# Five widths of a gather table in a hybrid decoder step: 34, 47, 37, 30, 11 columns become 33, 45, 34, 28, 10

## The chip, the cores and the metric

The kernel runs on one core of one Trainium2 chip. The metric is the device time of one execution in microseconds (us). The time before is 3196.83 us, the median of three runs from 3183.53 to 3199.43 us. All arithmetic is in 32-bit floats; most matrix products are made of three products of a high and a low part.

## The reference, cut to what matters

The program computes one layer of a decoder trunk for 512 prompt tokens and 64 sample tokens (8 sequences of 8), each of 2048 channels. The first half (modulation, a recurrent head group, a short convolution, an output projection) isn't touched. The second half is a mixture of 16,384 single-neuron experts, PEER:

```python
q = (xb @ w_q).reshape(PEER_BLOCK, PEER_HEADS, 2, HALF_DIM)
sc = jnp.einsum('thpk,pnk->thpn', q, sub_keys)
v1, i1 = lax.top_k(sc[:, :, 0], 16); v2, i2 = lax.top_k(sc[:, :, 1], 16)
cand = v1[..., :, None] + v2[..., None, :]        # 256 sums per head
top, pos = lax.top_k(cand, 16)
eidx = (i1 * 128 + i2) at pos                     # the expert
g = softmax(top)
act = gelu(sum_d x[d] * expert_u[eidx][d]) * g
out = sum over the picks of act * expert_v[eidx]
```

Each token has 8 heads of 16 picks: 128 picks, each of an expert whose number is first key times 128 plus second key. A pick takes a row of 2048 numbers (8 KB) of `u` and one of `v`.

## The kernel before, in words

**Two ways to an expert.** The 128 first keys are ranked by how often they are likely to be chosen (`rank_keys`, line 935). The experts of the first 80 keys (`L`, line 32), 80 blocks of 128 experts, are computed densely for all 512 prompt tokens: every token by every expert, with a weight of zero where the token didn't pick it. The picks of the other 48 first keys are gathered row by row, as are all 128 picks of the sample tokens.

**Dense part.** In the U stage TensorE runs over the 160 halves of the 80 `u` blocks (`u_half`, line 1395; its matmuls are line 1405). In the V stage it runs over 80 steps of four blocks each (`v_column`, line 1413; matmuls at line 1425). SyncE loads the raw halves (lines 892 and 897). ScalarE makes the high part `xhi` (line 908), GpSimd the low part `xlo` (line 909), and TensorE needs both.

**Gathered part.** `count` (line 1058) counts each prompt token's rare picks. `sort` (line 1113) orders the 512 tokens by that count, most first. The sorted tokens are cut into five tiles by `SORTED` (line 40): a first place, a number of tokens, and a number c of columns. With the sample tokens as tile 0 (64 columns, all full) they make the table `GT` (line 816). A tile of 128 tokens has one token on each partition and c slots for each. The first and the last tile have 64 tokens; each has its first c slots on one partition and the next c on another, so its token has 2c slots. `slots` (line 1187) fills the slots of a tile by taking the largest codes eight at a time, in rounds of eight (`mr`, line 1193). A slot that no pick fills gets an index past the end of the expert table, and the gather leaves out such a row.

**One column, one gather, one dot or one add.** For every column of the table `take` (line 1234) issues on GpSimd one indirect DMA of up to 128 rows of 8 KB. In `gather_u` (line 1238) VectorE then multiplies the landed rows by the token's input, which lies in PSUM, and sums (line 1263); in `gather_v` (line 1272) it multiplies by the activation and adds to an accumulator in PSUM (line 1290, the first of a tile 1287, the last 1292). The rows land in five buffers in the U stage and seven in the V stage.

**Order.** The whole of this is in an order written out by hand. In the U stage the dots of a tile follow as its slots become ready, at a set rate (line 1684); from the step at which all slots are ready the rest, and 16 adds of tile 0 (`EARLY_V`), are spread evenly over the steps that are left (line 1695). In the V stage the other adds are spread over the steps by a sum of costs: a column of tile 0 counts 1.25, any other 1.0 (lines 1753 and 1765). The tiles of the V stage come in the order 0, 2, 1, 3, 5, 4 (line 1315).

**What does not fit.** A token with more rare picks than slots is counted in `flag`:

```python
for i, (p0, n, c) in enumerate(GT):
    cap = c * 128 // n if i else NPK
    V.tensor_scalar(srt[:, i, 0:1], srt[:, i, 0:1], -float(cap), 0.0, op0=ALU.add, op1=ALU.max)
```

If the sum isn't zero, a general path at the end of the program (line 1813) goes through all five tiles once more, with 128 gathers of `u` and 128 of `v` for each, by the same `take`, keeps only the picks that had no slot, and computes the output again.

Of the kernel before, what the change touches and what calls it, by code (L numbers as in the profile page):

```python
# [36 lines left out]
TC = 32  # L37
NCH = NA // TC
QT = NA // 128
SORTED = ((0, 64, 34), (64, 128, 47), (192, 128, 37), (320, 128, 30), (448, 64, 11))  # L40
RB = 5
RV = 7
ENDS = 3
# [38 lines left out]
def build(ctx, tc, A, O, dbg=None):  # L82
# [732 lines left out]

    GT = [(None, NG, NPK // 2)] + [(p0, n, c) for p0, n, c in SORTED]
    rows_i, gwt = {}, {}
# [369 lines left out]
    def slots(i):  # L1187
# [5 lines left out]
        mr = -(-m // 8) * 8  # L1193
        sb = pools["rs"].tile([128, max(2 * NPK, 3 * max(-(-c_ * 128 // n_ // 8) * 8 for _, n_, c_ in SORTED))], F32,
                              name=f"sl{i}", tag="sl", bufs=1)
# [746 lines left out]
```

## Time and profile before

| | |
|---|---|
| median of three runs | 3196.83 us |
| the profiled execution | 3192.57 us |
| its span, first to last instruction | 3190.7 us |
| mean granted TensorE clock | 0.984 |
| gathers of `u` and of `v` | 223 and 223 |
| U stage, by the trace | about 1197 to 2214 us |
| V stage, by the trace | about 2214 to 3168 us |

A share is busy time over the span. A wait names the instruction that stood idle, the one that ended its wait, the total, how often, and the longest. A row of a stretch gives start and end, then the busy time of each engine and its count of instructions, the granted TensorE clock (1.00 is full), the mean busy share of the 16 DMA engines (a little over 1.00 where records overlap) and what they moved.

### The profile page before, as it was taken

The numbers are of one execution on the slowest core, as the hardware profiler recorded it, in microseconds if no ns is written. First come the engines' busy times: TensorE is split into PE (matmuls) and PEld (weight loads), VectorE is DVE, ScalarE is ACT, GpSimd is POOL, SyncE is SP. The second block draws the span as 40 slices with busy tenths as digits, with TensorE's granted clock in tenths as the row PEclk, the third lists the DMA queues.
The fourth block names the chain that finished last, engine by engine and source line by source line (L and its number), as shares of the span: only waits on it lengthen the run. The fifth ranks groups of instructions, "written<-read, shape, count | busy, mean of one in ns | idle before, by whom it ended". The sixth has DMA issues, their size and how long they took to land.

```text
span 3190.7 us, 46633 instructions
## 1 busy us (share of the span) xinstructions
PE 3063.3 (96%) x17239; PEld 2604.8 (82%) x17239; DVE 2151.6 (67%) x3267; ACT 1045.4 (33%) x1640; POOL 1708.0 (54%) x1001
## 2 busy tenths in 40 slices
PE   6999999999989999999999999998999999999997
PEld 2788888889979998887888788886888888777776
DVE  3455521142245897977898999856677888788755
ACT  3244311122232232232655555542322222222122
POOL 2233333344334235666666666656767777768642
PEclk9999999999999999999999999999999999999998
DMA  9744566633332227889879898989999999899964
GB/s 391 279 137 138 177 215 215 205 121 132 130 121 90 70 83 247 307 312 399 339 309 402 354 400 354 403 281 357 395 376 383 401 341 367 329 397 344 368 245 155
DMA packets 297067, 882.84 MB, mean 277 GB/s; under 512 B 37590, under 2 KB 79446, under 8 KB 245366
## 3 DMA queue, kind: packets, MB, share of 16 engines
q1 hardware_dynamic: 160608, 380.39, 34.0%
q0 software_dynamic: 66336, 413.41, 32.5%
q10 hardware_dynamic: 69888, 86.00, 7.6%
q8 instruction: 136, 2.23, 0.3%
q14 instruction: 99, 0.81, 0.1%
HBM read 879.89 MB, written 66.81 MB: 297 GB/s over the span
## 4 chain that ended last, share of the span: by engine, by line
PE 74%; DMA 12%; DVE 5%; POOL 3%; issue 3%; ACT 1%; SPq 0%; ACTq 0%; POOLq 0%; DVEq 0%
PE pu L1405 20%; PE pv L1425 19%; PE pp_o L140 6%; DMA raw<-v 3%; PE pp_c L140 3%; PE pp_s L140 3%; PE qa L140 3%; PE pp_b L140 3%; PE qb L140 3%; DMA gsb<-gd 3%; PE pp_x L140 2%; PE pp_y L140 2%; PE ada L190 2%; PE gbank L1605 2%; DMA v<-v,rows 2%
## 5 line engine op out<-in xcount | busy, mean ns | idle before, releaser
L909 POOL TENSOR_TENSOR xlo<-raw,xhi 128x1024 fp32r<-128x1024 f32 x320 | 778.6, 2444 | 408.7 <-ACT xhi L908 403.0
L908 ACT ACTIVATE xhi<-raw 128x1024 fp32r<-128x1024 f32 x320 | 338.1, 1060 | 875.4 <-PE pv L1425 319.8
L1263 DVE SCALAR_TENSOR_TENSOR u<-u,hT 128x2048 f32<-128x2048 f32 x223 | 503.7, 2282 | 111.3 <-DMA u<-u,rows 110.0
L1290 DVE SCALAR_TENSOR_TENSOR accB<-v,dots,accB 128x2048 f32<-128x2048 f32 x211 | 496.5, 2353 | 109.4 <-DMA v<-v,rows 103.2
L1425 PE MATMUL pv<-ahi,xhi 128*128 128x512 f32 x1280 | 511.5, 400 | 23.1 <-ACT xhi L908 16.2
L1405 PE MATMUL pu<-hhi,xhi 128*128 128x512 f32 x1280 | 514.4, 402 | 0.0
L1425 PE MATMUL pv<-ahi,xlo 128*128 128x512 f32 x1280 | 508.3, 397 | 4.3 <-POOL xlo L909 4.3
L1425 PE MATMUL pv<-alo,xhi 128*128 128x512 f32 x1280 | 506.0, 395 | 0.0
L1405 PE MATMUL pu<-hhi,xlo 128*128 128x512 f32 x1280 | 502.7, 393 | 0.4 <-POOL xlo L909 0.3
L1405 PE MATMUL pu<-hlo,xhi 128*128 128x512 f32 x1280 | 502.9, 393 | 0.0
L1235 POOL DMA_INDIRECT u<-u,rows x223 | 224.8, 1008 | 211.1 <-DVE u L1263 142.4
L1425 PEld LDWEIGHTS pv<-ahi,xhi 128*128 128x128 f32 x1280 | 243.2, 190 | 80.5 <-ACT xhi L908 17.5
L1425 PEld LDWEIGHTS pv<-ahi,xlo 128*128 128x128 f32 x1280 | 243.1, 190 | 63.0 <-POOL xlo L909 6.2
L1425 PEld LDWEIGHTS pv<-alo,xhi 128*128 128x128 f32 x1280 | 243.6, 190 | 55.2
L1235 POOL DMA_INDIRECT v<-v,rows x223 | 258.1, 1157 | 54.7 <-issue 39.5
L1405 PEld LDWEIGHTS pu<-hhi,xlo 128*128 128x128 f32 x1280 | 240.8, 188 | 56.2 <-POOL xlo L909 2.1
L1405 PEld LDWEIGHTS pu<-hhi,xhi 128*128 128x128 f32 x1280 | 241.4, 189 | 49.4 <-issue 0.9
L1405 PEld LDWEIGHTS pu<-hlo,xhi 128*128 128x128 f32 x1280 | 241.5, 189 | 48.4
L1599 ACT ACTIVATE op<-op,it 128x128 f32<-128x128 f32 x512 | 155.3, 389 | 35.6 <-DVE op L1591 32.8
L1605 PEld LDWEIGHTS gbank<-wr,op 128*128 128x128 f32 x1024 | 133.5, 192 | 24.0 <-ACT stg L1612 15.0
L129 POOL TENSOR_TENSOR wlo_o<-raw_o,whi_o 128x1024 fp32r<-128x1024 f32 x32 | 77.6, 2425 | 119.7 <-ACT whi_o L127 119.7
L1447 DVE TENSOR_TENSOR acc<-acc,pv 128x512 f32<-128x512 f32 x144 | 96.4, 681 | 65.7 <-PE pv L1425 63.6
(498 smaller groups left out, 5439.4 us busy)
## 6 DMA issues: line engine op xcount, KB each, us to landing
wa<-w_ada SPq DMA_DIRECT2D x96, 1024.0 KB
raw<-ut SPq DMA_DIRECT2D x160, 512.0 KB
raw<-v SPq DMA_DIRECT2D x320, 256.0 KB
actd<-act ACTq DMA_DIRECT2D x80, 256.0 KB
gd<-stg ACTq DMA_DIRECT2D x64, 320.0 KB
gsb<-gd ACTq DMA_DIRECT2D x80, 256.0 KB
actr<-actd ACTq DMA_DIRECT2D x40, 512.0 KB
raw_o<-w_out SPq DMA_DIRECT2D x32, 512.0 KB
```

The lines of the kernel that those rows point to most:

```text
L129: lo_engine(share).tensor_sub(lo, raw, r32(hi))
L140: PE.matmul(o, st, mv[pick](k), start=first, stop=last)
L908: S.activation(hi, raw, AF.Copy)
L909: G.tensor_sub(lo, raw, r32(hi))
L1235: G.indirect_dma_start(out=out, out_offset=None, in_=src, in_offset=bass.IndirectOffsetOnAxis(ap=idx, axis=0), bounds_check=NE * 128 - 1, ...
L1263: V.scalar_tensor_tensor(r, r, 1.0, st["h"], op0=ALU.mult, op1=ALU.mult, accum_out=dots[i][:, j:j + 1])
L1290: V.scalar_tensor_tensor(st["a"], r, dots[i][:, j:j + 1], st["a"], op0=ALU.mult, op1=ALU.add)
L1405: PE.matmul(pu, st[:, kk, :], movA[mv](k), start=k == 0 and a == 0, stop=k == KD - 1 and a == 2)
L1425: PE.matmul(pv, st, mv, start=first and j == 0 and a == 0, stop=last and not end and j == SG - 1 and a == 2)
L1447: V.tensor_add(ak, ak, pv)
L1599: S.activation(ops[:, j0 + j, :], ops[:, j0 + j, :], AF.Copy, scale=it[2][:, b * 4 + j:b * 4 + j + 1])
L1605: PE.matmul(pg[:, j * L:(j + 1) * L], ops[:, j0 + j, :], wr[:, j0 + j, :], start=True, stop=True)
```

## The change

```diff
-SORTED = ((0, 64, 34), (64, 128, 47), (192, 128, 37), (320, 128, 30), (448, 64, 11))
+SORTED = ((0, 64, 33), (64, 128, 45), (192, 128, 34), (320, 128, 28), (448, 64, 10))
```

Each tile keeps its tokens and loses one, two, three, two and one column. The slots of a token go from 68, 47, 37, 30, 22 to 66, 45, 34, 28, 20. All loops over the columns, the counts `NU`, `NV0` and `NT` that pace the gathers, and the bound `cap` follow from the table. Nothing else is edited.

## The prediction

> **What bounds the kernel.** I read the page from the top: the span, the busy times, the chain that ended last.
>
> ```profile
> span 3190.7 us, 46633 instructions
> ...
> PE 3063.3 (96%) x17239; PEld 2604.8 (82%) x17239; DVE 2151.6 (67%) x3267; ACT 1045.4 (33%) x1640; POOL 1708.0 (54%) x1001
> ...
> PE 74%; DMA 12%; DVE 5%; POOL 3%; issue 3%; ACT 1%; SPq 0%; ACTq 0%; POOLq 0%; DVEq 0%
> ```
>
> TensorE is busy for 3063.3 of 3190.7 us and makes 74% of the chain; VectorE and GpSimd, from which the change takes work, are busy 67% and 54%. But an average hides stages, so next come TensorE's own waits from 1180 us to the end, where the gathers run (the rows of the last few microseconds left out).
>
> ```profile
> PE pv L1425 <- ACT xhi L908: 16.2, 3, 8.8
> PE gbank L1605 <- ACT stg L1612: 8.9, 11, 3.3
> PE pv L1425 <- DVE acc L1447: 6.2, 4, 2.7
> PE pv L1425 <- POOL xlo L909: 4.3, 3, 1.6
> ...
> PE pv L1425 <- issue: 0.7, 1, 0.7
> PE pu L1405 <- POOL xlo L909: 0.3, 1, 0.3
> ```
>
> No row names a gather, a dot (L1263) or an add (L1290). The U stage's matmuls lose 9.2 us in all (8.9 + 0.3), the V stage's 27.4 us (16.2 + 6.2 + 4.3 + 0.7). These 36.6 us, and what the clock loses behind them, are all that any relief elsewhere could win here. Where do they lie? The view by stretches, cut at the ends of the gather's tiles:
>
> ```profile
> core 0: us, PE busy (x) PEld busy (x) DVE busy (x) ACT busy (x) POOL busy (x), PEclk, DMA share, GB/s
> ...
> 1853.00:2214.00 361.00, 360.13 (x1810) 302.69 (x1809) 289.98 (x312) 180.00 (x372) 222.49 (x145) 1.00 0.93 364
> 2214.00:2457.00 243.00, 231.42 (x989) 187.12 (x988) 174.25 (x96) 65.51 (x68) 168.07 (x95) 0.97 0.99 377
> 2457.00:2635.00 178.00, 178.00 (x774) 144.91 (x773) 150.46 (x90) 41.33 (x37) 135.00 (x81) 1.00 0.98 374
> 2635.00:2762.00 127.00, 126.14 (x546) 102.09 (x545) 104.56 (x62) 28.55 (x26) 92.18 (x58) 1.00 0.90 340
> 2762.00:2911.00 149.00, 141.56 (x597) 113.69 (x596) 120.39 (x74) 32.88 (x30) 109.00 (x67) 0.98 0.99 372
> 2911.00:2947.00 36.00, 36.00 (x157) 29.30 (x157) 31.05 (x19) 8.29 (x8) 30.44 (x19) 1.00 0.96 371
> 2947.00:3067.00 120.00, 112.45 (x470) 90.19 (x470) 96.17 (x55) 24.73 (x22) 79.15 (x48) 0.96 0.88 327
> ```
>
> From 1853 to 2214 us TensorE stands for 0.9 us of 361, though VectorE is at 80%. In the V stage it stands only in three stretches: 2214 (tile 0), 2762 (tile 3) and 2947 (tile 4). The DMA engines are at 0.88 to 0.99 throughout, the second resource near its end. Narrower, for TensorE alone:
>
> ```profile
> core 0: us, PE busy (x), PEclk, DMA share, GB/s
> 2224.00:2234.00 10.00, 5.75 (x13) 0.50 0.60 190
> 2234.00:2457.00 223.00, 223.00 (x967) 1.00 1.00 384
> 2780.00:2800.00 20.00, 17.30 (x69) 0.91 1.02 381
> 2820.00:2840.00 20.00, 16.42 (x70) 0.98 1.04 396
> 2980.00:3000.00 20.00, 14.66 (x55) 0.83 0.84 292
> 3000.00:3020.00 20.00, 17.80 (x71) 0.91 1.03 405
> ```
>
> The stops of tiles 3 and 4 lie near their heads, with the DMA share at 1.02 to 1.04 in three rows of four: raw blocks land late there. So the V stage is TensorE's, with DMA close behind.
>
> **What the change removes.** Nine columns, hence nine gathers of `u`, nine of `v`, and their dots and adds:
>
> ```profile
> L1263 DVE SCALAR_TENSOR_TENSOR u<-u,hT 128x2048 f32<-128x2048 f32 x223 | 503.7, 2282 | 111.3 <-DMA u<-u,rows 110.0
> L1290 DVE SCALAR_TENSOR_TENSOR accB<-v,dots,accB 128x2048 f32<-128x2048 f32 x211 | 496.5, 2353 | 109.4 <-DMA v<-v,rows 103.2
> ...
> L1235 POOL DMA_INDIRECT u<-u,rows x223 | 224.8, 1008 | 211.1 <-DVE u L1263 142.4
> ...
> L1235 POOL DMA_INDIRECT v<-v,rows x223 | 258.1, 1157 | 54.7 <-issue 39.5
> ```
>
> VectorE: 9 x 2.282 + 9 x 2.353 = 41.7 us. GpSimd: 9 x 1.008 + 9 x 1.157 = 19.5 us. Both lie beside TensorE, which hides them: the dots under U stage matmuls that lose 9.2 us in 1017, the adds under V stage matmuls. Were that cover gone, 41.7 us is the price (a rival below). The rounds that fill slots don't shrink: rounded up to eights, 68, 47, 37, 30, 22 give 72, 48, 40, 32, 24, and so do 66, 45, 34, 28, 20. Operations over c columns shrink by 1 to 3 elements: nothing.
>
> **What it doesn't remove: bytes.** Does an empty slot move data?
>
> ```profile
> q0 software_dynamic: 66336, 413.41, 32.5%
> ```
>
> This is GpSimd's queue. If each of the 446 gathers moved 128 rows of 8,192 bytes, they alone would make 467.7 MB. I worked the reference's routing out on its inputs (seed 0), ranking the first keys as the kernel does: the prompt has 16,261 rare picks. With tile 0's 128 x 64 = 8,192 slots that is 24,453 rows, twice 200.3 MB or 400.6 MB; the queue's other transfers, by their shapes (five reads of token inputs, the sums' writes, the codes), make 12.7 MB. The sum, 413.3 MB, is the row's 413.41 to within small packets. So empty slots (4,091 of 28,544, twice) move nothing to speak of, and the counts are the chip's. The same rows will move after: 413.4 MB, in 64 thousand packets or so.
>
> **What it moves: the pace.** In the V stage 207 adds are spread over the stretches above, 853 us (2214 to 3067), by cost: 48 x 1.25 + 159 = 219 units before, 210 after. A unit goes from 3.89 to 4.06 us: columns follow each other 4.1% more slowly. A tile's columns are full at its head and thin at its tail: tile 3's tokens have 34 to 28 rare picks, so 28 full columns, then thinning ones, and three of its 37 are empty. The change takes the empty ones off the tails and gives their time to the heads, where the stops lie. The stretches moved 309 MB (us times GB/s, summed); gathers are half of 413.4 less 12.7 for the others over two and 16 early columns, about 184 MB, 59%. 4.1% of 59% is 2.4% less traffic at the heads. Tile 3 has 28 full columns, 109 us, tile 4 has 20, 78 us: 2.4% of 187 us is **4.5 us** of lateness less. The four narrow rows there show 13.8 us of standing; a third of it goes. With it a third of the clock loss in those rows, (0.09 x 17.3 + 0.02 x 16.4 + 0.17 x 14.7 + 0.09 x 17.8) = 6.0 us, so **2 us**. Bounds: 0 if the raw blocks are late for another reason (a load of weights ahead of them), and all of 13.8 + 6.0 = 20 us if the lateness had only just crossed.
>
> In the U stage the 9 dots thin VectorE by 20.5 of 1017 us, 2%. TensorE waits there for ScalarE's copies (8.9 us), which wait at times for VectorE: I take **0.5 us**, between 0 and 9.2. The stop at the V stage's start (10 us at clock 0.50) belongs to the hand-over and tile 0, whose columns stay: 0, within plus or minus 12, the whole of it gone or once more.
>
> Sum: 4.5 + 2 + 0.5 = **7 us** off the profiled 3192.57, 3185.6; the three runs' median stands 4.3 us above the profiled execution, hence **3190 us**.
>
> One rule bears on the stops. The Trainium skill, "TensorE: Matmul & The Clock Gate", Part 1 (the HAM clock gate), says that the clock halves after an idle window of about 3.4 us. The row from 2224 to 2234 (0.50, after a wait of 8.8 us) agrees; by it alone a stop cut below that length would win all of its clock loss, and the sum would be 7 + 4 = 11 us.
>
> Another speaks against a gain. The same skill, "DMA: Bandwidth & Descriptors", "Where 436 GB/s comes from", says that HBM gives one core about 358 GB/s. The rows of 372 to 384 GB/s exceed that here; were it the bound, equal bytes would take equal time, the V stage would win nothing, and the sum would be 0.5 us.
>
> **The rivals.** *The stops go altogether*: the V stage's heads and start both come free, 20 + 12 us, 3164.9 us with the median's offset. For it: TensorE is at 178.00 of 178 us where DMA is at 0.98, so a small relief may be enough. Against: the start isn't touched. Chance 0.09.
>
> *VectorE's work is on the path*: all 41.7 us come off, 3155 us. For it: VectorE is at 80 to 85% in places. Against: the U stage row, 360.13 of 361 us. 0.03.
>
> *Something doesn't fit*: one token over its bound runs the general path, which nothing hides. That is 5 x 256 = 1,280 more gathers of full rows (an unused entry there reads row 0), 1.05 MB each; at 405 GB/s, the last row above, 2.6 us, more than a dot's 2.28 or an add's 2.35. 1,280 x 2.6 = 3,330 us: about 6,520 us. It decides from one pick over. The most rare picks at the heads of the tiles are, by my count, 65, 45, 34, 28, 20 against 66, 45, 34, 28, 20: four bounds are met exactly. For it: no slack. Against: the byte sum says that the chip picks as I count; and the count at each cut is shared by many tokens (45 by the sorted places 56 to 66, 20 by 445 to 452), so that the first token would have to gain two picks, or at least four tokens near a cut one each. Before, the same `take` ran 223 + 223 times, so nothing was over. 0.02.
>
> *The tails are missed*: the empty columns were pauses in which raw blocks caught up (shares 0.90 and 0.88 in the stretches of tiles 1 and 4). Without them each of two hand-overs, to tile 3 and to tile 4, gets a stop like the one after 2980 (5.3 us and 2.5 of clock): 16 us, 3213 us. It decides where the mean share passes 1.0; prompt tiles go from 159/219 to 150/210 of the time, 1.6% denser, and 0.99 x 1.01 at the worst is just 1.0. 0.07.
>
> **How the numbers follow.** The forecast has 0.79. About 0.5% (16 us) is what a measurement of this kernel can tell from no change. Faster by more: the first two rivals, 0.12, and 0.02 of the forecast's lower end. Slower by more: not fitting, 0.02, and half of the missed tails, about 0.03. Within: 0.81. The range goes from 3172 (half of the heads' bound and the start's stop, 16 to 18 us below 3190) to 3206 (a repeated start stop, 12 us, and the 4 us by which one run differs from another); it leaves out most of the rivals, 0.2.
>
> **What would show it.** Right: 214 + 214 gathers; the queue's bytes at 413.4 MB; TensorE's waits at L1425 down from 27.4 to some 20 us, the part before 2300 us much as it was; VectorE's busy time down by about 42 us with the span down by a sixth of that. Wrong in size: waits for `xhi` that vanish or double; a start of the V stage that moves the total more than the heads do. Wrong in kind: instructions of lines 1814 to 1870 in the trace, or a U stage that shortens by 20 us.

## The result, and the profile after

The changed kernel takes 3182.29 us (median of 5 runs, 3178.14 to 3187.19) against 3199.43 us of the kernel before (5 runs). The ratio is 0.995 with a 95% interval of 0.9929 to 0.9971. The forecast was 3190 us within 3172 to 3206 us. The profiled execution took 3178.14 us, its span is 3176.2 us.

From the page after: span, busy times, GpSimd's queue, and the groups of the dots and the adds (count, then busy time in us, mean in ns of one).

```profile
span 3176.2 us, 46544 instructions
...
PE 3060.1 (96%) x17239; PEld 2604.4 (82%) x17239; DVE 2123.5 (67%) x3240; ACT 1047.0 (33%) x1640; POOL 1681.4 (53%) x983
...
q0 software_dynamic: 63744, 413.40, 32.7%
...
L1263 DVE SCALAR_TENSOR_TENSOR u<-u,hT 128x2048 f32<-128x2048 f32 x214 | 483.2, 2282 | 104.3 <-DMA u<-u,rows 103.9
L1290 DVE SCALAR_TENSOR_TENSOR accB<-v,dots,accB 128x2048 f32<-128x2048 f32 x202 | 475.2, 2353 | 102.2 <-DMA v<-v,rows 99.0
```

The queue moved 413.40 MB where it had moved 413.41: no row went with the columns. (In tiles 2, 3 and 4 the columns that went were empty. In tiles 1 and 5, where a token's slots lie on two partitions, the rows of the column that went moved into the columns that stayed.) It has 2,592 packets fewer, 18 x 144. The dots' group is 20.5 us smaller and the adds' 21.3 us, 41.8 us together. VectorE has 27 instructions fewer (each dot is two, each add one: 18 + 9), GpSimd 18. TensorE's work is the same.

Where did 14.5 us of span go? The waits of TensorE after, from 1180 us (who waited for whom: total, times, longest; those of the last microseconds left out), to be set beside the six rows shown of before:

```profile
PE gbank L1605 <- ACT stg L1612: 7.6, 8, 2.3
PE pv L1425 <- POOL xlo L909: 6.2, 4, 1.7
PE pv L1425 <- DVE acc L1447: 5.4, 3, 3.5
...
PE pv L1425 <- ACT xhi L908: 2.6, 3, 1.5
...
PE pu L1405 <- POOL xlo L909: 1.5, 2, 1.2
```

The U stage loses 9.1 us (7.6 + 1.5) as before (9.2). The V stage loses 14.2 us (6.2 + 5.4 + 2.6) for 27.4. The views of the matmuls' groups give first and last start, so the length of a stage (before, then after):

```profile
L1425 PE MATMUL pv<-ahi,xhi x1280: 389/393/796, 2214.9 to 3165.3; 128*128 128x512 f32 x183
```

```profile
L1425 PE MATMUL pv<-ahi,xhi x1280: 387/393/797, 2219.6 to 3151.0; 128*128 128x512 f32 x183
```

The V stage went from 950.4 to 931.4 us, 19.0 us less: 13.2 of waits, and 5.8 of busy time for the same matmuls, which the higher granted clock behind shorter stops accounts for as far as its two digits tell (0.99 for 0.97 in the first stretch). The U stage's first matmul came at 1186.9 us before and 1192.5 after, so it took 1028.0 and 1027.1 us. The first half, which no edit touches, took 5.6 us more in the profile after; why isn't shown. The stretches after, cut again at the ends of the tiles:

```profile
core 0: us, PE busy (x) PEld busy (x) DVE busy (x) ACT busy (x) POOL busy (x), PEclk, DMA share, GB/s
2206.00:2461.00 255.00, 251.81 (x1079) 204.33 (x1078) 172.09 (x96) 69.15 (x71) 176.75 (x101) 0.99 0.99 374
2461.00:2637.00 176.00, 176.00 (x765) 143.26 (x764) 147.75 (x87) 41.21 (x37) 128.85 (x79) 1.00 0.98 370
2637.00:2772.00 135.00, 130.47 (x557) 105.54 (x556) 112.22 (x64) 28.77 (x26) 97.42 (x59) 0.98 0.90 340
2772.00:2908.00 136.00, 133.86 (x573) 107.78 (x572) 114.09 (x66) 30.86 (x28) 96.56 (x58) 0.99 1.00 382
2908.00:2945.00 37.00, 37.00 (x162) 30.09 (x162) 31.58 (x20) 8.06 (x7) 27.86 (x19) 1.00 1.00 391
2945.00:3053.00 108.00, 103.34 (x443) 82.58 (x442) 88.10 (x52) 24.85 (x23) 75.46 (x45) 1.00 0.95 360
```

TensorE stands for 3.2 us in the stretch of tile 0 (11.6 before), 2.1 in that of tile 3 (7.4), 4.7 in that of tile 4 (7.6), and for 4.5 us (0.9) in that of tile 1, at its end. So the start of the V stage won most, 8.4 us; the stretches of tiles 3 and 4 won 8.2 us, and the hand-over in front of tile 3 took 3.7 of it back.

What stopped the start before? ScalarE's wait for VectorE's weighing, from 2205 to 2245 us before and 2210 to 2250 after:

```profile
ACT ahi L1375 <- DVE actr L1368: 9.6, 1, 9.6
```

```profile
ACT ahi L1375 <- DVE actr L1368: 0.5, 1, 0.5
```

ScalarE splits the activations of a group of blocks (line 1375) after VectorE has weighed them (line 1368). In the kernel before it stood 9.6 us at that split, with the `xhi` of the next V matmuls behind it in its order: six V matmuls had run, the next waited 8.8 us. VectorE's side of it, the same instruction in the timeline, before and after (start, length, and in brackets its wait):

```profile
2221.78 2.29 DVE L1368 TENSOR_TENSOR actr<-actr,gsb 128x2048 f32<-128x2048 f32 x1 [7.29 <-DMA raw<-v]
```

```profile
2213.32 2.29 DVE L1368 TENSOR_TENSOR actr<-actr,gsb 128x2048 f32<-128x2048 f32 x1 [7.29 <-DMA actr<-actd]
```

In both a transfer ends the weighing's wait. Which one it was before is open: the row names a load of raw `v`, which the weighing doesn't read. Before, the weighing starts 6.9 us after the first V matmul (2214.9); after, 6.3 us ahead of it (2219.6).

### The profile page after: what moved, and what is told of

Its sections match the earlier page's. It is cut to its first block, busy times and chain, and to the rows that moved or that the text cites. A ratio compares the mean times of both kernels' runs of the same rounds, so it can differ in the third digit from the quotient of the medians.

```text
span 3176.2 us, 46544 instructions
## 1 busy us (share of the span) xinstructions
PE 3060.1 (96%) x17239; PEld 2604.4 (82%) x17239; DVE 2123.5 (67%) x3240; ACT 1047.0 (33%) x1640; POOL 1681.4 (53%) x983
## 3 DMA queue, kind: packets, MB, share of 16 engines
q0 software_dynamic: 63744, 413.40, 32.7%
## 4 chain that ended last, share of the span: by engine, by line
PE 68%; DMA 14%; POOL 6%; issue 5%; DVE 5%; ACT 1%; SPq 1%; ACTq 0%; POOLq 0%; DVEq 0%
PE pu L1405 17%; PE pv L1425 17%; PE pp_o L140 6%; DMA raw<-v 4%; DMA gsb<-gd 4%; PE pp_c L140 3%; PE pp_s L140 3%; POOL xlo L909 3%; PE qa L140 3%; PE pp_b L140 3%; PE qb L140 3%; PE pp_x L140 2%; PE pp_y L140 2%; PE ada L190 2%; DMA actr<-actd 2%
## 5 line engine op out<-in xcount | busy, mean ns | idle before, releaser
L1263 DVE SCALAR_TENSOR_TENSOR u<-u,hT 128x2048 f32<-128x2048 f32 x214 | 483.2, 2282 | 104.3 <-DMA u<-u,rows 103.9
L1290 DVE SCALAR_TENSOR_TENSOR accB<-v,dots,accB 128x2048 f32<-128x2048 f32 x202 | 475.2, 2353 | 102.2 <-DMA v<-v,rows 99.0
L1235 POOL DMA_INDIRECT u<-u,rows x214 | 214.7, 1003 | 206.5 <-DVE u L1263 154.2
L1235 POOL DMA_INDIRECT v<-v,rows x214 | 246.3, 1151 | 51.8 <-issue 33.9
L1447 DVE TENSOR_TENSOR acc<-acc,pv 128x512 f32<-128x512 f32 x144 | 96.9, 682 | 76.7 <-PE pv L1425 76.7
```

What stands on the lines that cost most here:

```text
L1235: G.indirect_dma_start(out=out, out_offset=None, in_=src, in_offset=bass.IndirectOffsetOnAxis(ap=idx, axis=0), bounds_check=NE * 128 - 1, ...
L1263: V.scalar_tensor_tensor(r, r, 1.0, st["h"], op0=ALU.mult, op1=ALU.mult, accum_out=dots[i][:, j:j + 1])
L1290: V.scalar_tensor_tensor(st["a"], r, dots[i][:, j:j + 1], st["a"], op0=ALU.mult, op1=ALU.add)
L1447: V.tensor_add(ak, ak, pv)
```

## The experiments

Three theories were put to the runs. A: in the V stage the columns follow each other more slowly (210 units of cost for 219), so raw blocks land in time at the heads. B: the end of the U stage is less crowded, 34 dots and adds in its last 30 steps (1.13 a step) for 38 in 28 (1.36), so that the weights and the first `v` blocks land in time. C: it is the engine time set free. In all tables "stops" is the sum of TensorE's waits at the V matmuls, and the V stage's length goes from the first to the last start of their first group; both come from one profiled execution, the ratio from all timed runs.

**One side at a time** (e2, e3). Columns that were taken out come back at the tails of their tiles with indices past the table, so that they move no rows, and with dots or multipliers that change nothing. The edit of e2, cut; e3 swaps the two pads and fetches `u` the same way:

```diff
...
+LESS = (0, 1, 2, 3, 2, 1)
+PAD_U, PAD_V = (0,) * 6, LESS
...
-            take(held[j][0], A["v"], rows_i[i][:, j:j + 1])
+            take(held[j][0], A["v"], rows_i[i][:, j:j + 1] if j < c else none)
...
-        for j in range(c):
+        for j in range(c + PAD_V[i]):
```

> The gathers and dots of u by the new table (214), those of v as many as before (223): the nine columns taken from v come back at the ends of their tiles as gathers whose indices all lie past the table, so they move no rows, and their adds multiply by zero. The V stage's pace by cost is that of before (219 units). Theory A (the V stage's slower pace thins the traffic at the heads of tiles 3 and 4): ratio to before 1.000, TensorE's waits at the matmuls of line 1425 about 27 us, the stop of some 9 us at the start of the V stage still there. Theory B (with fewer dots the end of the U stage is less crowded, so that the first v blocks land in time): that stop gone, ratio 0.997. Theory C (it is the engines' time itself, 41.7 us of VectorE and 19.5 us of GpSimd): about half of the whole gain of 0.5%, ratio 0.9975.

> The mirror image: v by the new table (214 gathers), u with nine empty columns put back (223). The V stage's pace is that of the changed kernel (210 units). Theory A: most of the gain, ratio 0.995 to 0.997, with the narrow stops at the heads of tiles 3 and 4 smaller. Theory B: the stop at the start of the V stage comes back, ratio 0.998. Theory C: half the gain, 0.9975.

**The places without the work, and the pace without the places** (e4, e5).

```diff
             uses.append(lambda j=j: add(j))
+        for _ in range(LESS[i]):
+            fetches.append(lambda: None)
+            uses.append(lambda: None)
```

```diff
-    cost = [FULL_ROWS if j < NU + bound[0] else 1.0 for j in range(NV0, NT)]
+    cost = [0.0 if j in pads else FULL_ROWS if j < NU + bound[0] else 1.0 for j in range(NV0, NT)]
```

> The new table, but each column taken out leaves an empty place in the hand-written order of u and of v: its gather, dot and add are gone, while the places of all others are those of before (223 and 223 places, 219 units). Theories A and B: the pace is that of before, so ratio 1.000 and TensorE's waits at line 1425 about 27 us. Theory C: the whole gain, ratio 0.995.

> All 223 and 223 gathers as before (nine empty columns put back in u and in v), but in the V stage the nine cost nothing in the sum that spreads the adds, so that the others go at the pace of the changed kernel (210 units). Theory A: ratio 0.996 to 0.998, the heads of tiles 3 and 4 as in the changed kernel. Theory B: the U stage is that of before, so the stop at the start stays, ratio 0.998 to 1.000. Theory C: no time is freed, ratio 1.000 or above.

| | ratio to before, 95% | stops, us | V stage, us |
|---|---|---|---|
| e2, new in U alone | 0.9942 (0.9923 to 0.9961) | 14.2 | 936.3 |
| e3, new in V alone | 0.9981 (0.9960 to 1.0002) | 11.5 | 932.3 |
| e4, places kept, work gone | 0.9965 (0.9949 to 0.9981) | 25.3 | 947.0 |
| e5, work kept, V pace new | 0.9981 (0.9964 to 0.9997) | 28.7 | 951.6 |

No theory held in all four. The U side alone gives as much as the whole change, which is B's, but more than B said, and with V's old pace the later stops shrank too. The V pace alone (e5) gives some 6 us, A's size (between 1 and 12 by the interval), though its profile shows none of it. With every place kept (e4) there is still a gain of 0.35%, which neither A nor B allowed: what went with the work (C's engine time, or the packets of 18 gathers) counts for a part. Of e3 the profiled execution, 3175.2 us, is the fastest of 12 whose median is 3192.96: its row is no guide to the ratio. One execution differs from another by some 10 us, so a single profile proves little.

**The two kernels once more** (f1, f2; no edit).

> The kernel before once more, for what one execution differs from another. Every theory: ratio 1.000 within 0.002. Theory B (the end of the U stage is too crowded: 38 dots and adds in its last 28 steps, 1.36 a step, against 34 in 30, 1.13, in the changed kernel) also says that the stop in the first 30 us of the V stage comes again, 5 us or more of it. If it was chance, this profile need not have it.

> The changed kernel once more, with more runs. Every theory: ratio 0.993 to 0.997. If the pieces of the first four runs add up (u side 0.9942, v side 0.9981), 0.992. Theory B: no stop over 4 us in the first 30 us of the V stage.

| | ratio to before, 95% | stops, us | V stage, us |
|---|---|---|---|
| f1, before again | 0.9997 (0.9984 to 1.0010) | 27.8 | 949.3 |
| f2, changed again | 0.9959 (0.9946 to 0.9972) | 16.1 | 930.9 |

TensorE's waits of f1 at the V matmuls, for the rows of before:

```profile
PE pv L1425 <- ACT xhi L908: 14.4, 3, 8.7
PE pv L1425 <- DVE acc L1447: 7.3, 5, 3.4
PE pv L1425 <- POOL xlo L909: 5.8, 4, 2.9
PE pv L1425 <- ACT acc L1445: 0.3, 1, 0.3
```

The stop of 8.8 us at the start is there again with 8.7, and the V stage's length comes again within 1.1 us in both kernels. The difference of 18 to 19 us in the V stage repeats, so it belongs to the kernels and not to one execution.

**Moving six adds across the border** (f3, f4). One number sets how many adds of tile 0 are made in the U stage: it crowds the U stage's end and thins the V stage, or the reverse, so A and B say the opposite of each other.

```diff
-EARLY_V = 16
+EARLY_V = 10
```

f3 is the kernel before with 10; f4 is the changed kernel with 22.

> The kernel before with 10 instead of 16 adds of tile 0 in the U stage: 32 dots and adds in its last 28 steps, 1.14 a step, the changed kernel's pace with all of the old work; the V stage gets six adds more (226.5 units for 219, so 3% denser). Theory A (pace of the V stage): slower than before, ratio 1.002. Theory B: the changed kernel's start of the V stage, ratio 0.995 to 0.998. Theory C (freed engine time): ratio 1.000.

> The changed kernel with 22 instead of 16 adds of tile 0 in the U stage: 40 dots and adds in its last 30 steps, 1.33 a step, about the pace of before (1.36); the V stage gets six fewer (202.5 units for 210). Theory A: a little faster than the changed kernel, ratio 0.993. Theory B: the stop at the start of the V stage is back, ratio 0.997 to 1.000. Theory C: as the changed kernel, 0.995.

f3: ratio 1.0047 (1.0028 to 1.0065), 15 us slower than before, V stage 968.3 us. f4: 0.9932 (0.9916 to 0.9948), 3176.56 us, against 3184.85 us of f2 on the same chip, V stage 931.1 us. Their waits at the V matmuls, f3 first:

```profile
PE pv L1425 <- ACT xhi L908: 17.3, 7, 4.4
PE pv L1425 <- POOL xlo L909: 15.1, 10, 2.5
PE pv L1425 <- DVE acc L1447: 8.0, 4, 3.5
```

```profile
PE pv L1425 <- ACT acc L1445: 8.6, 1, 8.6
PE pv L1425 <- POOL xlo L909: 3.7, 2, 2.0
...
PE pv L1425 <- ACT xhi L908: 2.4, 1, 2.4
PE pv L1425 <- DVE acc L1447: 1.9, 1, 1.9
```

Signs of both theories are seen in both runs. With 1.14 a step at the U stage's end (f3) the long stop at the start is gone, the longest wait anywhere is 4.4 us; but the waits, now 21 of them, have grown to 40.4 us with a V stage only 3% denser. With 1.33 a step (f4) a long stop is back, 8.6 us, some 23 us into the V stage, but at another place: TensorE waits for ScalarE's copy of a finished sum (L1445), not for `xhi`. All the others together are 8.0 us. In the total the V stage's density decides: six gathers into it cost 15 us, 2.5 us each; six out of it win 8.3 us, 1.4 us each. B alone as the cause, and C alone (1.000 for f3), fall.

**Levers by themselves, and together** (g1, g4, g2). g1 spreads the changed kernel's V adds by the rows that a column is likely to hold. g4 is the kernel before with the last U steps drawn to the front. g2 is the changed kernel with both, and 22 early adds. The cuts of the edits:

```diff
-    cost = [FULL_ROWS if j < NU + bound[0] else 1.0 for j in range(NV0, NT)]
...
+    order_ = [x for i in VO[1:] for x in fills[GT[i][0]]]
+    cost = [FULL_ROWS] * (NU + bound[0] - NV0) + [FULL_ROWS * max(0.55, x) for x in order_]
...
-            gather_to(G0 + (NU + EARLY_V - G0) * (n - R2) // (NU2 - 1 - R2))
+            x_ = (n - R2) / (NU2 - 1 - R2)
+            gather_to(G0 + (NU + EARLY_V - G0) * x_ * (1.3 - 0.3 * x_) + 1e-6)
```

`fills` is 1 up to the next tile's number of slots and falls in a line to 0 at the tile's own.

> The changed kernel, with the V stage's adds spread by the rows that a column is likely to hold: a full column of any tile counts 1.25 as one of tile 0 does, a thin one down to 0.69; 227 units instead of 210. A full column of tiles 2, 3 and 4 then comes every 4.7 us instead of 4.06 (13% fewer rows at a time), one of tile 0 7% more often. Theory A (traffic at the heads): TensorE loses next to nothing at the heads of tiles 3 and 4, ratio to the kernel before 0.991 to 0.993. Theory B (only the crowding of the U stage's end counts): as the changed kernel, 0.995. Theory C (freed engine time): 0.995.

> The kernel before, with the 38 dots and adds in its last 28 U steps drawn to the front: from 1.76 a step down to 0.95 a step instead of 1.36 throughout. All work, all columns and the V stage's pace are those of before. Theory B: the stop at the start of the V stage goes, ratio 0.996 to 0.998, and the V stage's later stops stay near 25 us in sum; if the late start is carried on through the stage, they shrink too and the ratio is 0.994. Theory A and theory C: 1.000.

> All levers together: the changed kernel, 22 adds of tile 0 in the U stage drawn to its front (40 in 30 steps, from 1.73 a step down to 0.93), and the V stage's adds spread by rows. Theories A and B together: no stop over 4 us at the start, next to none at the heads, ratio 0.988 to 0.990. Theory C: 0.995.

| | ratio to before, 95% | stops, us | V stage, us |
|---|---|---|---|
| g1, V by rows | 0.9967 (0.9953 to 0.9982) | 22.4 | 937.4 |
| g4, before, U end drawn forward | 0.9984 (0.9967 to 1.0001) | 20.8 | 941.3 |
| g2, both and 22 early adds | 0.9894 (0.9871 to 0.9917) | 2.0 | 911.4 |

g4 loses half of the start's stop (4.3 us for 8.8) and little time. g1 didn't do what A said: a stop of 8.9 us came at the start, where tile 0's columns are 7% denser, and of the later ones some 11 us stayed. All three levers together clear the stage: 3158.27 us, 24 us below the changed kernel and 38 below the kernel before. Of that the six early adds alone were worth 8.3 us (f4); the other two weren't run together without them. Its stretches, TensorE alone (length, busy, clock, DMA share, GB/s):

```profile
core 0: us, PE busy (x), PEclk, DMA share, GB/s
2216.00:2460.00 244.00, 241.91 (x1047) 1.00 1.01 381
2460.00:3053.00 593.00, 593.00 (x2589) 1.00 0.95 359
```

TensorE doesn't stand once in 593 us. The queue's bytes are those of the changed kernel, 413.40 MB, with six gathers moved ahead into the U stage: spread more evenly, they fit beside the matmuls.

**The V stage's first 60 us, and the rest, run by run.** For each profile: the units of cost over which the V adds are spread, the dots and adds a step at the U stage's end, and TensorE's waits at the V matmuls in us, first 60 us (the longest in brackets) and later.

| | units | a step | first 60 us | later |
|---|---|---|---|---|
| before | 219 | 1.36 | 11.6 (8.8) | 15.8 |
| f1, before again | 219 | 1.36 | 10.2 (8.7) | 17.6 |
| e3, new in V alone | 210 | 1.36 | 3.4 (1.7) | 8.1 |
| e4, places kept, work gone | 219 | 1.36 | 8.1 (5.7) | 17.2 |
| e5, work kept, V pace new | 210 | 1.36 | 13.2 (8.3) | 15.4 |
| g4, before, U end drawn forward | 219 | 1.76 to 0.95 | 7.6 (4.3) | 13.2 |
| f4, changed, 22 early | 202.5 | 1.33 | 12.7 (8.6) | 3.9 |
| changed | 210 | 1.13 | 3.2 (1.7) | 11.0 |
| f2, changed again | 210 | 1.13 | 5.0 (1.7) | 11.0 |
| e2, new in U alone | 219 | 1.13 | 5.0 (1.8) | 9.2 |
| f3, before, 10 early | 226.5 | 1.14 | 3.8 (2.4) | 36.6 |
| g1, V by rows | by rows | 1.13 | 11.7 (8.9) | 10.7 |
| g2, all three | by rows | 1.73 to 0.93 | 2.0 (1.4) | 0.0 |

A crowded end of the U stage goes with a long stop at the start, a thin one with none, but not always: e3 is as crowded as before and has no stop, g1 is thin and has one. Nor is it one and the same stop. Only before and f1 weigh the activations late, 6.9 and 5.0 us after the first V matmul. In e3, e4 and e5, just as crowded, the weighing starts 4.6 to 5.0 us ahead of it; the long stops of e4, e5, f4, g4 and g1 are waits for ScalarE's copies. So what delayed the weighing before isn't shown. The later stops follow the units in f3 and f4, but e2 has fewer of them at the old pace, and e5 as many as before at the new one. The weighing's rows of f1 (first V matmul at 2217.5) and e5 (2217.3):

```profile
2222.51 2.29 DVE L1368 TENSOR_TENSOR actr<-actr,gsb 128x2048 f32<-128x2048 f32 x1 [7.96 <-DMA raw<-v]
```

```profile
2212.26 2.29 DVE L1376 TENSOR_TENSOR actr<-actr,gsb 128x2048 f32<-128x2048 f32 x1
```

**One column too few** (g3).

```diff
-(64, 128, 45)
+(64, 128, 44)
```

> The changed kernel with one column less in tile 2 (44 for 45): tokens with 45 rare picks have one too many, so the general path runs. By the prediction's price 1,280 gathers of full rows at 2.6 us: 3,182 + 3,330, about 6,510 us; if its gathers don't overlap with its dots, 1,280 x (2.6 + 2.3), about 9,450 us. By the count of picks it must run; if it doesn't, the count is wrong and the time is that of the changed kernel.

6564.94 us, one execution. From its page: the queue, and the groups of the general path.

```profile
q0 software_dynamic: 249328, 1765.71, 65.9%
...
L1845 DVE SCALAR_TENSOR_TENSOR f_a<-f_v,f_d,f_a 128x2048 f32<-128x2048 f32 x640 | 1504.7, 2351 | 115.1 <-DMA f_v<-v,f_ri 37.0
...
L1843 DVE SCALAR_TENSOR_TENSOR f_u<-f_u,f_h 128x2048 f32<-128x2048 f32 x640 | 1466.5, 2292 | 153.5 <-DMA f_u<-u,f_ri 152.2
L1235 POOL DMA_INDIRECT f_v<-v,f_ri x640 | 1395.3, 2180 | 227.5 <-issue 189.6
L1235 POOL DMA_INDIRECT f_u<-u,f_ri x640 | 1371.2, 2142 | 250.5 <-issue 197.0
```

640 + 640 gathers, 1,352 MB more than in the changed kernel. It is 3,383 us slower than the changed kernel's 3182.29, 2.64 us a gather. The table of the change is the tightest that fits: one column less costs 200 times what the change won.

## Why the prediction was right, point by point

The median of 3182.29 us lies inside the range, but the gain, 17 us (13 us in the runs of f2), is about twice the 7 us that the sum gave.

**No empty slot moves bytes: right.** 413.40 MB, and 64 thousand packets. **Fit to the last slot: right**, and the price of a miss, 6,520 us, came out as 6564.94.

**The cover of the engines' work: mostly right.** 41.8 us left VectorE's two groups and 14.5 us the span, a third, where a sixth was forecast. VectorE's total fell by only 28.1 us: the low halves of the activations (L1379) took 8.2 us more than before and smaller groups the rest, and no run shows why. Work alone (e4) still counts for some of the gain, where nothing was allowed.

**The U stage, 0.5 us: right for the stage itself, and the wrong place to look.** It took 0.9 us less in the first pair of profiles and 1.3 less in the second, less than the 1.8 us between two executions of the kernel before. But the new table in U alone (e2) gives as much as the whole change, and its V stage is 14.1 us shorter (936.3 for 950.4). The prediction had no term for what fewer dots in the U stage do to the V stage behind it.

**The heads, 4.5 us: met in size, not shown in kind.** The stretches of tiles 1, 3 and 4 stand 4.6 us less in sum (0.9 + 7.4 + 7.6 before, 4.5 + 2.1 + 4.7 after). That it comes out at 4.6 is in part luck: tiles 3 and 4 won 8.2 us and the hand-over in front of tile 3 lost 3.7. That stop is the rival of the missed tails, at 3.7 us instead of its 16. Nor were all these stops late raw blocks, as the prediction held: 6.2 us of the 15.8 after the first 60 us were waits for VectorE's sums (L1447), and 5.4 stayed; the waits for `xhi` fell from 7.4 to 1.1 us, and those for `xlo` rose from 1.5 to 4.5. f3 and f4 show that the density of the V stage can set such stops, and e5, the pace by itself, wins some 6 us in its timed runs; but the stops of e5's profile are those of before, and those of e2 shrank at the old pace. So the pace may have been the cause here, and the runs don't settle it. The clock was to win 2 us; the V stage's busy time fell by 5.8.

**The start, "0, within plus or minus 12": this term was mis-sized.** The prediction held that it "belongs to the hand-over and tile 0, whose columns stay". The columns stay, and the stop went: the stretch won 8.4 us, and up to 4.4 us of clock (0.03 x 231.4 before, 0.01 x 251.8 after). That is most of what lies between the forecast's 7 us and the 17 us measured; the range had been drawn wide enough for it. f1 and f2 show the start's stop and its absence a second time. What removed it is shown in part: e2, with the U stage's end thinned and V as before, loses the stop. With nine dots fewer, the U stage's tail starts two steps sooner, and spreads 34 entries over 30 steps where it had 38 over 28. But e3 loses the stop too, with 38 over 28, and e5 has a different one, so the crowding alone isn't the cause.

**The rule that HBM gives one core about 358 GB/s** (the Trainium skill, "DMA: Bandwidth & Descriptors", "Where 436 GB/s comes from") would have left the V stage as it was. It shrank by 19 us with the same bytes, at 374 to 391 GB/s in its fullest stretches, with one core at work; so the measurement decides against it as a bound here.

**What stays open.** Why the weighing came late before, and which part of the later stops the pace removed, isn't settled. The parts don't add: U alone and V alone make 0.9942 x 0.9981 = 0.992, the change 0.995 and 0.9959. Which of the later stops appear shifts with each edit (g1 kept two that A had struck off), and how much of e4's gain is VectorE's time, how much GpSimd's and how much the empty gathers' packets wasn't tried apart.

## What to carry to other kernels

An entry that does no work still has a place in a hand-written order: when the pace is drawn from counts, taking empty places out moves all the others, and so the waits at every stage border, also in the stage behind. Where two resources are both near full (here TensorE at 100% and the DMA engines at 0.88 to 0.99), ask of an edit what it does to the densest 100 us, and to the steps just ahead of a stage's start, before counting the work it removes. A bound set to the data's exact maximum wins half a percent and risks a doubling: such a table holds for these inputs alone.

## What the runs showed of the hardware

A gather with no valid row isn't free for the queues. The nine such gathers of e2 added 1,296 packets to the changed kernel's 63,744, 144 each, as many as its 128 rows and 16 more, and hardly a byte (413.41 MB for 413.40).

In the general path GpSimd took 2.14 to 2.18 us to issue a gather, in the stages of the kernel before 1.01 to 1.16. There VectorE's multiplications have both inputs in SBUF, and the DMA engines were busy for 0.99 of the time; in the stages one input is in PSUM. The Trainium skill, "SBUF — State Buffer", "SBUF: two separate sides", says that a GpSimd operation that reads SBUF and a VectorE operation with two SBUF inputs share a port pair that one holds at a time. The longer issues would fit that; no run separated it from other causes, such as the full queues.

With the DMA engines busy 95% of the time TensorE ran for 593 us without a single stop (g2), while the same rows and an estimated 6 MB more (six gathers of 1.05 MB) in the V stage, less evenly spread, cost the kernel before 27 us of stops.
